# Deferring the norm of the first six tiles to the copies out of PSUM, and spreading the FFN weights' write-backs, in a hybrid decoder layer

## The chip, the cores and the metric

The kernel runs on all 8 cores of one Trainium2 chip. The time is device microseconds (us) of the slowest core. Four cores share a die. A run is called slow when one die is over 1% longer than the other at a lower granted clock, or when the run is over 1.5% above the fastest of the same kernel; such runs occur with many of the kernels here and are left out of all comparisons. Every experiment was timed in rounds with the kernel before on the same chip.

## The reference, cut to what matters

```python
h = rmsnorm(x, g_mix)                 # x * rsqrt(mean(x*x) + eps) * g
proj = h @ w_in                       # q, k, v (512 each), u and qm (256 each)
# three groups of heads read proj: dilated window attention (q, k, v),
# a pooling mixer (u), cross-attention into 256 memory tokens (qm)
x = x + concat(y_attn, y_pool, y_mem) @ w_out
x = x + relu(rmsnorm(x, g_ffn) @ w_ff1) ** 2 @ w_ff2
return rmsnorm(x, g_final)
# x (4, 8192, 1024) float32, D_FF = 4096
```

Each core computes 8 own tiles of 512 tokens. For the window attention it first needs K and V of the 4 tiles that come before them (halo tiles 0 to 3). Tiles 4 to 11 are the core's own.

## The kernel before

The matmuls (PE) take bf16. Weights lie in DRAM as float32 and come in pieces: on first use a piece is loaded with a cast by a DMA of POOL's queue (`ring<-wall`, 2 MB read, 1 MB written), then written back as bf16 by SP's queue (`wscratch<-ring`); later uses load the bf16 copy, again from SP's queue (`ring<-wscratch`, 1 MB). Three slots (the ring) hold the piece in use and two ahead. PE (matmuls; PEld are its weight loads), ACT, DVE and POOL (element by element work) and SP (issues DMAs) each work off one queue in program order; `T.op` and `T.dma` add the waits for semaphores. PE writes to PSUM, from which ACT or DVE copies the result out.

```python
class LN:                                       # cut
    def square(self, k):                        # ACT squares chunk k, DVE adds it to acc
        ...
    def stat(self):                             # PE: mean over features by a float32 matmul with ones
        m_, bm_ = next_mm()
        mm_ops(m_, bm_, [(ones, self.acc, ...)])
        # ACT: acc = exp(-0.5 * ln(m + eps))
    def norm(self, k):                          # DVE: h[k] = x[k] * g[k] * acc
        ...

# ... cut: projections of tile j read h; a copy out of PSUM follows each group of 8 matmuls
for j in range(NHALO):                          # halo tiles
    nxt = stage_A(j + 1)
    side = ln_side(nxt, 0, 0.5, 4, 4.5, 0.5)    # squares, stat, norm of the next tile, between the groups
    groups = stage_B(j)
    if j == 3:                                  # keys and values of the memory tokens
        mln, mg = mem_groups()
        side += ln_side(mln, 2.2, 0.5, 6.2, 6.7, 0.4)
        groups += mg
    run(groups, side)

# V's rows take a turn through DRAM to be permuted; POOL waits for all four and reads them back
def read_v():
    for t_ in toks:
        T.wait("pool", t_)
    T.dma("pool", vsr_sem[j % 2], Vd4[...], vs[...])

# plan of the weights: 18 pieces are cast in the first own tile, 8 of them again in the second
deferred = {P_FF1 + i for i in range(1, 8, 2)} | {P_FF2 + i for i in range(1, 8, 2)}
def ring_issue():
    # ... cut
    if idx in done:
        T.dma("sp", ring_sem[s], ring[s][:], sc[idx], ...)
    else:
        T.dma("pool", cast_sem[s], ring[s][:], wall[idx], ...)
        if idx in deferred:
            deferred.discard(idx)
            return                              # no write-back this time
        done.add(idx)
        T.dma("sp", wb_sem[s], sc[idx], ring[s][:], ...)   # SP waits here until the cast has landed
```

The softmax here doesn't subtract the row's maximum and nothing guards it: scores larger than these inputs give would overflow.

## Time and profile before

Before: median 1656.29 us (3 runs, 1654.83 to 1660.23). The profiled run is core 1, the slowest. The page's head, busy times, chain and DMA issues ("us to landing" is the median from issue to landing):

```profile
span 1660.2 us, 27812 instructions; the slowest of 8 cores (1640.5 to 1660.2 us)
PE 1548.5 (93%) x9722; PEld 748.0 (45%) x9722; DVE 930.2 (56%) x1383; ACT 715.5 (43%) x1069; POOL 137.2 (8%) x189
...
PE 80%; DMA 7%; DVE 5%; issue 4%; ACT 4%; ACTq 0%; DVEq 0%; POOL 0%; SPq 0%; POOLq 0%
...
ring<-wscratch SPq DMA_DIRECT2D x142, 1024.0 KB, 5.9
ring<-wall POOLq DMA_DIRECT2D x29, 1024.0 KB, 12.0
```

PE is busy 93% of the span and 80% of the chain that ended last. The gain has to come from PE's idle time and from time at a lower clock. The waits of PE show the idle time (total, times, longest):

```profile
PE mm L336 <- DVE acc L362: 38.9, 8, 19.5
PE mm L336 <- DVE X L709: 15.9, 13, 1.5
PE mm L336 <- DMA ring<-wall: 9.9, 3, 4.7
PE mm L336 <- DMA ring<-wscratch: 9.4, 2, 7.3
```

39 us are waits for sums of squares (`acc`), of which 19.5 come before the first tile; 19 us are waits for weights. The timeline of PE shows the start (start, duration, what, in brackets the idle time before and what ended it):

```profile
19.53 2.05 PE L336 MATMUL mm<-acc,ones 128*128 128x512 f32 x2 [19.53 <-DVE acc L362]
24.05 11.38 PE L336 MATMUL mm<-ring,hT 128*128 128x512 bf16 x32 [2.48 <-DVE hT L374]
38.06 2.05 PE L336 MATMUL mm<-acc,ones 128*128 128x512 f32 x2 [2.62 <-DVE acc L362]
...
115.39 7.07 PE L336 MATMUL mm<-hT,ring 128*128 128x512 bf16 x32
...
147.96 0.60 PE L554 MATMUL sc<-QM,kmT 64*128 64x512 bf16 x4
```

The first projection is at 24.05 us, the first own tile's at 115.39, and its attention (`sc<-QM`) starts at 147.96.

### The profile page before, as it was taken

Reading aid. Unit: us, or ns where it says so; the run is one execution under the profiler, and the core shown is the slowest. Engines: PE = TensorE matmul, PEld = TensorE weight load, DVE = VectorE, ACT = ScalarE, POOL = GpSimd, SP = SyncE. Lnnn points to the kernel's source line nnn. Section 1 sums busy time; section 2 is a strip of 40 time slices with the busy share of each in tenths; the row PEclk is TensorE's granted clock in tenths of the full one; section 3 lists DMA queues with packets and bytes.
Section 4 is the critical chain, followed back from the end, with each engine's and each line's share of the span. In section 5 each row is a group of like instructions: output and inputs, shape, how many; then the busy total and the mean of one; then the engine's idle time right before and its main releaser. Section 6 shows DMA issues by size and latency. Waiting matters only on the chain.

```text
span 1660.2 us, 27812 instructions; the slowest of 8 cores (1640.5 to 1660.2 us)
## 1 busy us (share of the span) xinstructions
PE 1548.5 (93%) x9722; PEld 748.0 (45%) x9722; DVE 930.2 (56%) x1383; ACT 715.5 (43%) x1069; POOL 137.2 (8%) x189
## 2 busy tenths in 40 slices
PE   3889899989799999999999999999999999998996
PEld 1434544444355444454454444454445444453442
DVE  5666566546365466656465556656565555546333
ACT  3545654532444336443444436343444335442221
POOL 1102110101000010000100010000100000000000
PEclk9999999999999999999999999999999999998998
DMA  9828578995857675354835375344734373434342
GB/s 227 227 87 263 131 153 165 198 203 174 245 152 201 180 219 200 105 176 138 276 107 178 110 233 178 128 153 166 253 114 167 128 234 122 163 130 152 139 152 90
DMA packets 41081, 282.93 MB, mean 170 GB/s; under 512 B 5248, under 2 KB 5376, under 8 KB 8560
## 3 DMA queue, kind: packets, MB, share of 16 engines
q1 hardware_dynamic: 24048, 172.01, 30.6%
q0 software_dynamic: 16896, 109.13, 25.6%
q8 instruction: 81, 1.33, 0.3%
q14 instruction: 56, 0.46, 0.1%
HBM read 266.77 MB, written 46.92 MB: 189 GB/s over the span
## 4 chain that ended last, share of the span: by engine, by line
PE 80%; DMA 7%; DVE 5%; issue 4%; ACT 4%; ACTq 0%; DVEq 0%; POOL 0%; SPq 0%; POOLq 0%
PE mm L336 70%; PE ob L577 6%; PE sc L554 4%; DMA ring<-wall 3%; DMA ring<-wscratch 2%; ACT P L556 2%; DVE acc L362 1%; ACT sq L360 1%; DMA wscratch<-ring 1%; DVE val L588 1%; DMA out<-X 1%; DVE X L709 1%; DVE X L374 0%; DMA cpc_t<-cpc 0%; ACT rt L686 0%
## 5 line engine op out<-in xcount | busy, mean ns | idle before, releaser
L336 PE MATMUL mm<-h2T,ring 128*128 128x512 bf16 x2192 | 511.0, 383 | 13.9 <-DMA ring<-wscratch 7.3
L336 PE MATMUL mm<-aT,ring 128*128 128x512 bf16 x2048 | 474.2, 382 | 24.5 <-DVE X L709 15.9
L689 DVE TENSOR_TENSOR aT<-rt 128x512 bf16<-128x512 f32 x256 | 199.9, 783 | 242.6 <-ACT rt L686 241.1
L556 ACT ACTIVATE P<-sc 128x1024 bf16<-128x1024 f32 x256 | 247.7, 1023 | 184.4 <-PE sc L554 178.7
L336 PEld LDWEIGHTS mm<-h2T,ring 128*128 128x128 bf16 x2192 | 206.7, 98 | 256.3 <-issue 32.7
L336 PEld LDWEIGHTS mm<-aT,ring 128*128 128x128 bf16 x2048 | 192.6, 98 | 249.5 <-issue 42.8
L686 ACT ACTIVATE rt<-mm 128x512 f32<-128x512 f32 x256 | 153.0, 598 | 272.2 <-PE mm L336 250.7
L561 DVE TENSOR_TENSOR P<-P,E 128x1024 bf16<-128x1024 bf16 x224 | 154.0, 694 | 127.6 <-ACT P L556 126.5
L360 ACT ACTIVATE sq<-X 128x512 f32<-128x512 f32 x196 | 122.4, 630 | 161.3 <-DVE X L709 102.5
L362 DVE TENSOR_TENSOR acc<-acc,sq 128x512 f32<-128x512 f32 (+1 forms) x203 | 142.9, 705 | 73.6 <-ACT sq L360 71.1
L336 PE MATMUL mm<-hT,ring 128*128 128x512 bf16 x704 | 156.3, 383 | 0.5 <-DVE KT L343 0.5
L709 DVE TENSOR_TENSOR X<-X,mm 128x512 f32<-128x512 f32 x128 | 87.6, 685 | 119.2 <-PE mm L336 118.6
L577 PE MATMUL ob<-P,Vd 128*128 128x128 bf16 x1792 | 136.7, 219 | 9.6 <-DVE val L588 7.8
L577 PEld LDWEIGHTS ob<-P,Vd 128*128 128x128 bf16 x1792 | 116.1, 98 | 64.9 <-issue 20.9
L592 POOL TENSOR_TENSOR yT<-val,den 128x512 bf16<-128x512 f32 x48 | 62.4, 1300 | 772.6 <-DVE val L588 240.0
L336 PE MATMUL mm<-yT,ring 128*128 128x512 bf16 x512 | 114.8, 383 | 2.7 <-POOL yT L592 2.1
L336 PEld LDWEIGHTS mm<-hT,ring 128*128 128x128 bf16 x704 | 69.2, 99 | 87.2 <-issue 8.2
L336 PEld LDWEIGHTS mm<-yT,ring 128*128 128x128 bf16 x512 | 49.8, 98 | 68.4 <-issue 12.3
L374 DVE SCALAR_TENSOR_TENSOR h2T<-X,gc,acc 128x512 bf16<-128x512 f32 x88 | 61.7, 745 | 27.8 <-ACT acc L370 23.5
L554 PE MATMUL sc<-Q,KT 64*128 64x128 bf16 x1792 | 71.8, 219 | 2.0 <-ACT P L556 1.3
L588 DVE COPY val<-ob 64x512 f32<-64x512 f32 x96 | 65.9, 687 | 13.1 <-PE ob L577 11.1
L336 PE MATMUL mm<-ring,hT 128*128 128x512 bf16 x288 | 68.6, 389 | 3.1 <-DVE hT L374 2.5
(70 smaller groups left out, 785.1 us busy)
## 6 DMA issues: line engine op xcount, KB each, us to landing
ring<-wscratch SPq DMA_DIRECT2D x142, 1024.0 KB, 5.9
ring<-wall POOLq DMA_DIRECT2D x29, 1024.0 KB, 12.0
X<-xh POOLq DMA_DIRECT2D x24, 1024.0 KB, 10.5
wscratch<-ring SPq DMA_DIRECT2D x21, 1024.0 KB, 7.3
X<-xr POOLq DMA_DIRECT2D x16, 1024.0 KB, 7.1
out<-X POOLq DMA_DIRECT2D x16, 1024.0 KB, 9.9
Vd<-vscratch POOLq DMA_DIRECT2D x10, 768.0 KB, 7.8
vscratch<-Vd POOLq DMA_DIRECT2D x32, 192.0 KB, 7.1
```

Of the source, the lines that this page charges most:

```text
L336: T.op("pe", lambda: nc.tensor.matmul(out_ap, lhsT=l, rhs=r, start=(i == 0), stop=(i == n - 1)), reads=rd, writes=[b_out], mark=(i == n - 1))
L360: T.op("act", lambda: nc.scalar.activation(out=s_, in_=self.x3[:, k, :], func=AF.Square), reads=[self.b_x[k]], writes=[bs_])
L362: T.op("dve", lambda: nc.vector.tensor_tensor(out=self.acc, in0=self.acc, in1=s_, op=ALU.add), reads=[bs_], writes=[self.b_acc])
L554: T.op("pe", lambda: nc.tensor.matmul(o2, lhsT=l[lo:lo + 64], rhs=rr, start=True, stop=True), reads=bt["qk_reads"], writes=[bs_], mark=(i ...
L556: T.op("act", lambda: nc.scalar.activation(out=P_[:], in_=s_[:], func=AF.Exp, scale=0.125), reads=[bs_], writes=[bP_])
L561: T.op("dve", lambda: nc.vector.tensor_tensor(out=Pv, in0=Pv, in1=m, op=ALU.mult), reads=[bP_, b_E, b_E16], writes=[bP_])
L577: T.op("pe", lambda: nc.tensor.matmul(o_, lhsT=l[:, v0:v0 + 128], rhs=r_, start=(bt["first"] and i == 0), stop=(bt["last"] and i == n - 1) ...
L588: T.op("dve", lambda: nc.vector.tensor_copy(out=val[lo:lo + 64, :], in_=ob[hh][lo:lo + 64, :]), reads=[b_ob[hh]], writes=[b_val[hh]])
L592: T.op("pool", lambda: nc.gpsimd.tensor_tensor(out=yT[:, ch, :], in0=val[:], in1=den[:], op=ALU.mult), reads=b_den + b_val, writes=[b_yT[ch]])
L686: T.op("act", lambda: nc.scalar.activation(out=rt[i][:, 0:TOK], in_=m_[:], func=AF.Relu), reads=[bm_], writes=[b_rt[i]])
L689: T.op("dve", lambda: nc.vector.tensor_tensor(out=aT[:, a_, :], in0=rt[i][:, 0:TOK], in1=rt[i][:, 0:TOK], op=ALU.mult), reads=[b_rt[i]], w ...
L709: T.op("dve", lambda: nc.vector.tensor_tensor(out=xi[:, d, :], in0=xi[:, d, :], in1=m_[:], op=ALU.add), reads=[bm_], writes=[bxi[d]])
```

## The change

It has two halves.

1. The start. The projections of tiles 0 to 5 take x times the gain, with no norm, so that PE need not wait for the sum of squares. The reciprocal norm is multiplied in at the copies out of PSUM: along the free axis for K, Q and U (DVE, `tensor_tensor` with acc), per partition for V (ACT's scale), for which four one-column float32 matmuls per tile (the column statistics) make a column form of the norm. V of a halo tile runs chunk by chunk, a third input buffer lies in `aT`, V's weights load first, the memory tokens' work moves into the first own tile, and there the pooling mixer's additions go from DVE to POOL.
2. The plan of weights. Instead of 10 write-backs in the first own tile and 8 in the second there are 4, 5, 5 and 4 in the first four, at the price of 19 more cast loads. The load of the next x moves from step 11.7 to 17.

The diff, cut to its core:

```diff
-        deferred = {P_FF1 + i for i in range(1, 8, 2)} | {P_FF2 + i for i in range(1, 8, 2)}
+        turn = dict(zip([P_FF1 + i for i in range(4)] + [P_FF2 + i for i in range(4)]
+                        + [P_FF1 + 4 + i for i in range(4)] + [P_FF2 + 4 + i for i in range(4)],
+                        [2, 1, 3, 2, 1, 0, 3, 2, 1, 3, 1, 2, 3, 0, 2, 1]))
 ... (ring_issue)
+            T.dma("pool", cast_sem[s], ring[s][:], wall[idx], writes=[b_ring[s]])
+            if turn.get(idx, 0) == j - NHALO:
                 done.add(idx)
                 T.dma("sp", wb_sem[s], sc[idx], ring[s][:], reads=[b_ring[s]], writes=[b_scp[idx]])
 ... (LNEarly, the norm of tiles 0 to 5)
+            def gain(self, k):      # even k: ACT, out3[k] = x[k] * g; odd k: DVE
+            def stat(self):
+                for b in range(4):
+                    mm_ops(ob[0][:, b:b + 1], b_ob[0], [(a4[:, b, :], ones[:, 0:1], ...)])
+                ... (ACT: col = exp(-0.5 * ln(ob + eps)))
+                LN.stat(self)
 ... (copies out of PSUM, tiles 0 to 5)
+                T.op("act", lambda: nc.scalar.activation(out=d4[:, :, 0::2, :], in_=src, func=AF.Copy,
+                                                         scale=rcol[j % 2][:, b:b + 1]), ...)     # V
+                    T.op("dve", lambda: nc.vector.tensor_tensor(out=out, in0=m_, in1=a_, op=ALU.mult), ...)
 ... (pool_steps)
+                e = "pool" if first_own else "dve"
+                ops.append(lambda: T.op(e, lambda: T.eng[e].tensor_tensor(out=out, in0=in0, in1=in1, op=ALU.add), ...
 ... (first own tile)
+        side = [(0.5, lns[j].stat)]
+        side += [(8, ... write_back(p_) for p_ in (P_V, P_K, P_UM, P_Q)])]
+        side += ln_side(mln, 1, 0.4, 5, 5.5, 0.4)
+            side += gains(lns[j + 1], 8, 0.6) + sums(lns[j + 1], 8.3, 0.6) + [(16, lns[j + 1].stat)]
+        side += [(4 + 0.7 * i, f) for i, f in enumerate(pool_steps(j))]
+        run(stage_B(j) + mg, side)
 ... (own tiles)
-                side += [(11.7, lambda j=j: load_x("pool", (j + 1) % 2, xh[j + 2]))]
+                side += [(17, lambda j=j: load_x("pool", (j + 1) % 2, xh[j + 2]))]
```

A number before a step is its place in a list: step 8 is issued ahead of the group of matmuls with index 8.

## The prediction

> **What bounds it now.** PE is busy 93% of the span (page, part 1) and is 80% of the chain of waits. From 560 to 1500 us it is busy 923 of 940 us (windows): nothing to win there. The loss is in two places.
>
> (a) The start. The PE timeline of core 1 has the first projection at 24.05 us; halo tiles and memory keys end at 115.4; attention of the first own tile starts at 147.96. At 1.73 us per group of eight matmuls the projections are about 91 us of PE. PE waits for the sum of squares 32 us: 19.5 before the first tile, 2.4 to 4.1 in each later one, because squares, sums, statistic and normalisation stand in line. DMA isn't the limit after the first tile: four 2 MB inputs landed by 31.8 us, about 6.3 us each, then input loads waited for buffers (POOL behind hT, 39 us).
>
> (b) The first two own tiles. Waits for weights on core 1: 1.9, 4.7, 3.3, 7.3, 2.1 us between 341 and 548; other cores 7 to 18 us in all. Cast loads take 12 us in the median, up to 20, with write-backs beside them. After such gaps the granted clock was 0.5 for 3.4 to 10 us. "TensorE: Matmul & The Clock Gate", Part 1, of the Trainium skill says that the gate halves the clock after an idle window of 3.4 us; the trace agrees. Such stretches cost core 1 some 8 us more.
>
> **What changes.** Projections start from x times gain (one short op per chunk); the norm is applied when PSUM is copied out; V runs chunk by chunk. V's weights load first. At 6.3 us each I expect them at about 12.5 us, x's halves at 15.7 and 19, K at 25, the second x at 32, the third at 38. The first projection starts near 16.5 instead of 24. Then PE should run nearly gapless: 13.9 us per halo tile plus about 1.7 for statistics (four one-column fp32 matmuls are added to the 1.1 us one). Memory keys (4 us) move into the first own tile. Halo ends near 89, attention starts at 125 to 130 instead of 148. I take off some, because in the first own tile nearly all PSUM copies go to DVE (about 0.7 us each, beside sums, gains and memory norms), and pool sums to POOL (1.3 us each). Gain: 19 us (14 to 25).
>
> Write-backs: 10 in the first own tile become 4; in exchange 19 more cast loads (2 MB read, not 1) in own tiles two to four. DMA share is 0.5 to 0.7 there, so most hide; some may land late beside input loads. Moving the x load from step 11.7 to 17 takes it away from the store. I expect weight waits and slow clock to fall by half to two thirds on the slow cores: 15 us (3 to 22).
>
> Attention, FFN and the end keep their work.
>
> **Time.** 1656 - 19 - 15 = 1622 us, range 1606 to 1640. Faster by over 2% (below 1623.2): 0.54; within 2%: 0.44; slower: 0.02.
>
> **What would show it.** First projection near 16.5 us; PE waits for sums below 5 us after it; attention of the first own tile at 125 to 130; waits for weights below 8 us on the slowest core, none over 4; at most two steps of clock 0.5 between 100 and 500; 48 casts instead of 29, and no new waits for weights after 560; the end's length unchanged.
>
> **What would make it wrong.** PE waits for DVE in the first own tile (K and Q copies late); slow one-column fp32 matmuls; POOL's small copies at the start delaying the third halo input; cast loads of tiles two and three landing late, which turns (b) into new waits.

## More of the kernel before

In each own tile the pieces come in this order: W_out 0 and 1, the projections V, K, Q, U of the next tile, then FF1 pieces 0 to 3, FF2 0 to 3, FF1 4 to 7, FF2 4 to 7. When a piece has been used up, the piece three places on is issued into its slot.

The weight waits stand in the first two own tiles. This part of the chain is at the border between projections and FFN in the second (start, duration, what):

```profile
412.95 9.27 DMA out<-X
...
423.33 12.24 DMA ring<-wall
...
435.64 0.32 SPq L100
...
436.12 15.29 DMA ring<-wscratch
...
451.65 4.51 PE mm L336 x14
```

It reads: a store of the last tile lands; then POOL issues a cast load (FF1 piece 1), which lands 12.24 us later; only then does SP issue that piece's write-back, and behind it the load of piece 2; PE gets piece 2 at 451.65.

## The result, and the profile after

The changed kernel took 1681.71 us (median of 4 runs; three fast ones at 1679.03 to 1684.28 and a slow one at 1830.0) against 1658.26 for the kernel before (4 runs). The ratio is 1.0137, 95% interval 1.0102 to 1.0173. Ratios here and below are the mean time of one kernel's fast runs over that of the other's of the same rounds, so they are not quite the ratios of the medians. The prediction of 1622 (1606 to 1640) was wrong in sign.

The same views of the slowest core, again core 1, first the page:

```profile
span 1678.1 us, 27902 instructions; the slowest of 8 cores (1659.5 to 1678.1 us)
PE 1556.4 (93%) x9770; PEld 757.5 (45%) x9770; DVE 924.1 (55%) x1363; ACT 718.0 (43%) x1079; POOL 160.2 (10%) x230
...
PE 78%; DMA 8%; DVE 5%; ACT 4%; issue 4%; POOL 0%; ACTq 0%; DVEq 0%; POOLq 0%; SPq 0%
...
ring<-wscratch SPq DMA_DIRECT2D x123, 1024.0 KB, 5.6
ring<-wall POOLq DMA_DIRECT2D x48, 1024.0 KB, 10.8
```

48 cast loads instead of 29, as foreseen. Each takes a little less in the median, 10.8 us. The waits of PE:

```profile
PE mm L353 <- DMA ring<-wall: 19.8, 5, 6.7
PE sc L353 <- ACT hT L411: 17.9, 1, 17.9
PE mm L353 <- DVE X L816: 15.9, 13, 1.5
PE mm L353 <- DVE KT L582: 13.8, 6, 7.9
PE mm L353 <- DMA ring<-wscratch: 9.5, 1, 9.5
PE mm L353 <- DVE acc L384: 6.6, 2, 4.0
```

The waits for sums at the start are gone but for 5.3 us under other names (2.8 for the column statistics, 2.5 for the memory tokens); the 6.6 us shown stand at the end of the kernel, and stood there before. New are 13.8 us for copies of K out of PSUM, one of 7.9 us, and the waits for weights grew from 19 to 29 us. The timeline of PE at the start:

```profile
17.86 9.25 PE L353 MATMUL sc<-ring,hT 128*128 128x512 bf16 x32 [17.86 <-ACT hT L411]
26.99 2.00 PE L353 MATMUL ob<-ones,acc 128*128 128x1 f32 x8
28.85 1.11 PE L353 MATMUL mm<-acc,ones 128*128 128x512 f32 x2
...
44.44 2.00 PE L353 MATMUL ob<-ones,acc 128*128 128x1 f32 x8 [0.67 <-DVE acc L384]
...
81.24 0.95 PE L353 MATMUL ob<-ones,acc 128*128 128x1 f32 x8
...
100.58 1.89 PE L353 MATMUL sc<-hT,ring 128*128 128x512 bf16 x8
...
139.38 6.46 PE L353 MATMUL mm<-hT,aT 128*128 128x512 bf16 x16 [7.89 <-DVE KT L582]
...
155.09 0.61 PE L660 MATMUL sc<-QM,kmT 64*128 64x512 bf16 x4
```

The first own tile's projections begin at 100.58 instead of 115.39, but its attention only at 155.09 instead of 147.96: 54.5 us for a stretch that took 32.6 before (there without the memory tokens, whose matmuls are about 5 us). Now split the span by stage. The first projection of own tile j's output (`yT,ring`) marks the beginning of a tile's stage I; the table has the mean over the 8 cores of the profiled run, in us, worked out from the trace.

| | before | after |
|---|---|---|
| attention of first own tile starts | 147.5 | 153.4 |
| its output projection starts | 201.1 | 206.7 |
| from there to the second tile's | 171.9 | 169.1 |
| second to third | 198.1 | 198.3 |
| third to fourth | 185.1 | 202.4 |
| each later tile but the last | 185.1 to 185.4 | 185.1 to 185.2 |
| mean span of the cores | 1649.1 | 1669.3 |

So of 20.2 us, 5.9 come from the start, 17.3 from the third own tile, and the first own tile gave 2.8 back. The rows from the second tile on run to the output projection of the next tile, so "third" covers output projection and FFN of own tile 3, with the projections of tile 4 between them.

Where the start loses can be added up. From the first projection to the attention of the first own tile, mean of the 8 cores, before took 123.0 us and after 135.1:

| | before | after | cost |
|---|---|---|---|
| PE idle | 16.8 | 20.0 | +3.2 |
| PE busy at granted clock 0.5, after the first clock record | 7.5 | 12.2 | +2.4 (half of it) |
| PE busy before the first clock record, taken as half speed too | 7.3 | 4.5 | -1.4 (half) |
| the six tiles' column statistics, at full clock | 0 | 7.9 | +7.9 |
| the ordinary statistics, at full clock (before, tile 0's lies ahead of this stretch) | 4.7 | 5.6 | +1.0 |
| all other matmuls, at full clock | 94.1 | 93.3 | -0.9 |
| sum | | | +12.2 |

The head start was 6.2 us (first projection at 24.5 before and 18.3 after, mean of the cores), and 6.2 less 12.2 is the loss of about 6. The largest entry is the column statistics. In tiles 3 to 5 they took 0.95 to 0.97 us, in tiles 0 to 2 2.00 us (1.81 once), on every core, and the granted clock was 1.0 when they began. What differs in the program is the operand: in tiles 0 to 2 the matmul takes every fourth column of `acc` as its weights, later a contiguous block, and a weight load took 327 ns there against 192 later. No run tested another layout, or left the column statistics out.

The Trainium skill, "TensorE: Matmul & The Clock Gate", Part 1, says that the array runs at half clock after at least one idle window of about 3.4 us. This trace agrees in the sizes (records of 0.5 for 3.4, 6.8 and 10.2 us), but such records also came after much less idle time. On core 1 the clock was 0.5 from 46.2 us on, and in the 3.4 us before PE had been idle for 0.67 us only, while column statistics took 1.76. Of the 15 records of 0.5 before 75 us on the eight cores, 8 came like this: under 1 us idle, and 1.6 to 2.0 us of column statistics. So these may cost clock as well as time; that is seen side by side in the trace and not tested.

The chain through the longest wait at the start:

```profile
123.51 8.76 DMA vscratch<-Vd
...
132.81 0.54 POOL Vd L100
...
133.41 1.07 POOL rt L711
...
137.08 1.27 POOL rt L711
...
138.44 0.06 DVE rt L727
...
138.54 0.70 DVE KT L582
...
139.38 6.48 PE mm L353 x16
```

V's last rows take 8.76 us to land in DRAM. POOL waits for them (`read_v`), and only then reaches the pooling additions (`rt`), the last of which ends at 138.35. DVE's next instruction needs their result. Behind it in DVE's queue stands K's copy, which has nothing to do with pooling, and PE waits for that copy's PSUM buffer.

And the chain at the border in the third tile:

```profile
614.43 15.78 DMA ring<-wall
...
630.29 0.32 SPq L100
...
630.76 18.72 DMA ring<-wscratch
...
649.73 5.59 PE mm L353 x16
```

It is the pattern of before, one piece earlier. FF1 piece 0 (turn 2) is now a cast load from POOL's queue. Its slot was free when K's last group ended, near 611.1 us (worked out: the 96 matmuls of K, Q and U took 20.88 us from 604.14 on, K's are the first third), but POOL issued the load at 614.43, behind its wait for V's rows (landed at 612.27), their read-back and a store; the load then ran beside that store and the x load, and landed after 15.78 us, 4.8 us late for PE. Its write-back waited for it in SP's queue, and behind the write-back stood the load of piece 1, which was issued at 630.76 and landed 18.72 us later: another 9.5 us. In the kernel before, piece 0 at the same place in the second tile came as bf16 from SP's queue: by the trace it was issued at 409.80 and landed at 415.59. So the cast load is late by its issue (3.3 us) and by its own length (15.78 us, 10.8 in the median); no run separates the two.

### The profile page after: what moved, and what is told of

The parts are those of the page before. It is cut to its first block, busy times and chain, and to the rows that moved or that the text cites. A ratio compares the mean times of both kernels' runs of the same rounds, so it can differ in the third digit from the quotient of the medians.

```text
span 1678.1 us, 27902 instructions; the slowest of 8 cores (1659.5 to 1678.1 us)
## 1 busy us (share of the span) xinstructions
PE 1556.4 (93%) x9770; PEld 757.5 (45%) x9770; DVE 924.1 (55%) x1363; ACT 718.0 (43%) x1079; POOL 160.2 (10%) x230
## 3 DMA queue, kind: packets, MB, share of 16 engines
q0 software_dynamic: 19632, 129.05, 32.6%
## 4 chain that ended last, share of the span: by engine, by line
PE 78%; DMA 8%; DVE 5%; ACT 4%; issue 4%; POOL 0%; ACTq 0%; DVEq 0%; POOLq 0%; SPq 0%
PE mm L353 66%; PE ob L683 6%; DMA ring<-wall 5%; PE sc L660 4%; PE sc L353 2%; ACT P L662 2%; DMA ring<-wscratch 1%; DMA vscratch<-Vd 1%; DVE val L694 1%; DMA X<-xh 1%; DVE acc L384 1%; DMA out<-X 1%; DVE X L396 1%; DVE X L816 1%; DVE h2T L396 1%
## 5 line engine op out<-in xcount | busy, mean ns | idle before, releaser
L353 PE MATMUL mm<-h2T,ring 128*128 128x512 bf16 x2192 | 516.5, 385 | 31.5 <-DMA ring<-wall 14.7
L796 DVE TENSOR_TENSOR aT<-rt 128x512 bf16<-128x512 f32 x256 | 202.4, 792 | 261.4 <-ACT rt L793 260.1
L353 PE MATMUL mm<-hT,ring 128*128 128x512 bf16 x672 | 147.0, 379 | 2.6 <-DVE KT L582 2.5
L384 DVE TENSOR_TENSOR acc<-acc,sq 128x512 f32<-128x512 f32 x144 | 104.4, 725 | 41.2 <-ACT sq L374 40.5
L353 PEld LDWEIGHTS mm<-hT,ring 128*128 128x128 bf16 x672 | 65.4, 98 | 83.0 <-issue 6.2
L694 DVE COPY val<-ob 64x512 f32<-64x512 f32 x96 | 65.9, 687 | 12.7 <-PE ob L683 10.7
L660 PEld LDWEIGHTS sc<-Q,KT 64*128 64x128 bf16 x1792 | 53.6, 107 | 40.0 <-issue 36.7
L692 ACT ACTIVATE den<-ob 64x512 f32<-64x512 f32 x96 | 56.8, 592 | 29.4 <-PE ob L683 27.4
## 6 DMA issues: line engine op xcount, KB each, us to landing
ring<-wall POOLq DMA_DIRECT2D x48, 1024.0 KB, 10.8
```

The lines of the kernel that those rows point to most:

```text
L353: T.op("pe", lambda: nc.tensor.matmul(out_ap, lhsT=l, rhs=r, start=(i == 0), stop=(i == n - 1)), reads=rd, writes=[b_out], mark=(i == n - 1))
L384: T.op("dve", lambda: nc.vector.tensor_tensor(out=self.acc, in0=self.acc, in1=s_, op=ALU.add), reads=[bs_], writes=self.b_acc)
L660: T.op("pe", lambda: nc.tensor.matmul(o2, lhsT=l[lo:lo + 64], rhs=rr, start=True, stop=True), reads=bt["qk_reads"], writes=[bs_], mark=(i ...
L694: T.op("dve", lambda: nc.vector.tensor_copy(out=val[lo:lo + 64, :], in_=ob[hh][lo:lo + 64, :]), reads=[b_ob[hh]], writes=[b_val[hh]])
L796: T.op("dve", lambda: nc.vector.tensor_tensor(out=aT[:, a_, :], in0=rt[i][:, 0:TOK], in1=rt[i][:, 0:TOK], op=ALU.mult), reads=[b_rt[i]], w ...
```

## The experiments

The theories. For the start, R1: the order in POOL's queue, as just read, blocks DVE and through it PE. R2: DVE itself is too full in the first own tile, since nearly all copies out of PSUM are now DVE's. R3: POOL and DVE hinder each other. For the third tile, T1: the wrong pieces are cast at the border, where POOL's and SP's queues are blocked. T2: 19 more cast loads simply overload DMA.

Results, with the mean over the cores of the attention's start and of own tiles 1 to 3 from the profiled run. The first two lines are the first measurement. The kernel before, in the rounds of b1 to b4, has one run of 1678.31 among others of 1656.53 to 1658.35; it counts as fast, widens these four intervals and lowers their ratios by about 0.2%.

| run | mean of fast runs | ratio to before (95%) | attention | tiles 1, 2, 3 |
|---|---|---|---|---|
| before | 1658.0 | 1 | 147.5 | 171.9, 198.1, 185.1 |
| changed | 1680.8 | 1.0137 (1.0102 to 1.0173) | 153.4 | 169.1, 198.3, 202.4 |
| e1_sums_dve | 1672.1 | 1.0079 (1.0059 to 1.0098) | 150.4 | 168.5, 197.1, 202.9 |
| e2_sums_pool_early (wrong) | 1676.7 | 1.0106 (1.0082 to 1.0129) | 153.7 | 169.1, 197.6, 203.1 |
| e3_old_turns | 1664.9 | 1.0035 (1.0013 to 1.0057) | 153.2 | 172.2, 198.2, 185.4 |
| e4_turns_permuted | 1649.3 | 0.9950 (0.9918 to 0.9981) | 153.5 | 169.1, 185.3, 187.6 |
| b1_before_ring | 1668.9 | 1.0052 (0.9979 to 1.0124) | 147.7 | 167.1, 196.3, 203.1 |
| b2_before_ring_permuted | 1640.9 | 0.9878 (0.9819 to 0.9937) | 147.5 | 167.1, 185.8, 189.0 |
| b3_permuted_sums_dve | 1646.2 | 0.9910 (0.9849 to 0.9971) | 151.3 | 168.3, 186.5, 189.9 |
| b4_permuted_pool_early | 1647.4 | 0.9917 (0.9846 to 0.9988) | 152.3 | 168.1, 185.2, 188.5 |
| e6_writeback_late | 1677.5 | 1.0100 (1.0080 to 1.0120) | 151.1 | 168.1, 199.9, 204.4 |
| v1_balanced | 1643.1 | 0.9896 (0.9872 to 0.9920) | 146.2 | 168.7, 185.6, 189.4 |
| v2_balanced_plain5 | 1646.7 | 0.9914 (0.9889 to 0.9940) | 150.1 | 166.8, 186.2, 189.7 |
| b5_before_ring_spread | 1638.6 | 0.9866 (0.9847 to 0.9885) | 148.4 | 167.5, 185.3, 185.2 |
| h1_after_late | 1673.1 | 1.0080 (1.0058 to 1.0103) | 154.9 | 169.8, 199.6, 196.5 |
| h4_one_swap | 1658.9 | 1.0001 (0.9981 to 1.0021) | 154.8 | 169.4, 193.5, 186.7 |
| h3_b5_late | 1637.7 | 0.9867 (0.9851 to 0.9883) | 147.9 | 167.3, 185.7, 185.2 |
| h2_v1_spread_late | 1639.4 | 0.9878 (0.9858 to 0.9898) | 146.8 | 169.0, 185.8, 185.2 |

### e1_sums_dve: the pooling additions back on DVE

```diff
-                e = "pool" if first_own else "dve"
+                e = "dve"
```

> The changed kernel with one edit: the additions of the pooling mixer for the first own tile go back from POOL to DVE. Theory R1 (order in POOL's queue): in the changed kernel four additions stand in POOL's queue behind a wait for the landing of V's rows in DRAM (132.8 us), DVE's in-order queue waits for them (7.3 us idle), and with it K's copy out of PSUM, so PE stands 7.9 us and then runs at half clock for 10 us. Without it that wait is gone, attention of the first own tile starts at 140 to 146 us instead of 149 to 157, and the kernel is 8 to 12 us faster than the changed one (about 1671). Rival R2 (DVE is overloaded in this tile, since it now makes nearly all copies out of PSUM): DVE gets 4 us more work, attention starts at 155 or later, total the same or some us longer.

The total fell by 9 us and, by ratio, by 0.6%; the mean over the cores fell by only 4.1 (1669.3 to 1665.2), of which the attention's start gives 3.0. The 7.9 us wait for K is gone; its slowest core waits like this between 95 and 160 us:

```profile
PE mm L353 <- DVE KT L582: 5.3, 5, 1.3
PE mm L353 <- DVE val L384: 2.6, 1, 2.6
PE mm L353 <- DVE dT L733: 1.5, 1, 1.5
PE mm L353 <- DVE Q L582: 1.2, 2, 0.6
```

Five waits for K now make 5.3 us, none over 1.3. So R1 holds for the one long wait, but the attention started at 148 to 154 us, not at 140 to 146: more than half of R1's expected gain came back as short waits for a DVE with more to do, as R2 has it.

### e2_sums_pool_early: the additions on POOL, but earlier in its queue

```diff
-        side += [(4 + 0.7 * i, f) for i, f in enumerate(pool_steps(j))]
+        side += [(4 + 0.2 * i, f) for i, f in enumerate(pool_steps(j))]
```

> The changed kernel with one edit: the pooling steps of the first own tile are emitted closer together (0.2 instead of 0.7 of a group apart), so that POOL's additions stand in its queue before the wait for V's rows, and stay on POOL. R1 (queue order): the same gain as with the additions on DVE, attention starts at 140 to 146 us, total 8 to 12 us less than the changed kernel. R2 (DVE overload): attention start unchanged within 2 us, 149 to 157. Rival R3 (POOL and DVE slow each other when both read SBUF): the variant with DVE gains, this one doesn't.

The result was wrong (relative error 0.042), by a mistake of mine: the two map matmuls among the steps write into the tile that still holds the memory tokens, and at the closer spacing they came before those had been read. Nor did it gain at the start: the attention began at 152 to 156 us, because the maps now stood early in PE's queue, where PE waited 9.6 us for their operand. The wait had only moved. It decides nothing between R1 and R2; b4 mends it.

### e3_old_turns: the write-backs as before, the rest as changed

```diff
-                        [2, 1, 3, 2, 1, 0, 3, 2, 1, 3, 1, 2, 3, 0, 2, 1]))
+                        [0, 1, 0, 1, 0, 1, 0, 1, 0, 1, 0, 1, 0, 1, 0, 1]))
```

> The changed kernel with the old plan of write-backs (even FFN pieces in the first own tile, odd ones in the second; no cast loads later); everything else stays. T1 (head of line: a write-back waits in SP's queue for a late cast load and holds up the next weight load) and T2 (plain DMA overload by 19 more cast loads) both expect the third own tile back at 185 us from 199 to 205, the first own tile up by 0 to 8 us on some cores, the second within 5 us. Total 8 to 14 us less than the changed kernel, about 1670.

As expected: the third tile is back at 185.4, the first rises by 3.1, the second stays. The total fell by some 16 us, 2 more than expected. What is left over before (ratio 1.0035) is the start. This run keeps the x load at step 17, so with the old plan of weights that move by itself costs nothing.

### e4_turns_permuted: the same counts, other pieces

```diff
-                        [2, 1, 3, 2, 1, 0, 3, 2, 1, 3, 1, 2, 3, 0, 2, 1]))
+                        [0, 0, 1, 1, 1, 1, 1, 2, 3, 3, 2, 2, 3, 3, 2, 2]))
```

> The changed kernel with the same number of cast loads and write-backs in each own tile (2, 5, 5, 4 written back), but other pieces: FF1 pieces 0 and 1, the first after the border between projections and FFN, are written back in the first own tile, pieces 2 and 3 in the second, so that in the third tile the first pieces come from the bf16 copy. T1 (head of line at that border): third own tile 185 to 190 us instead of 199 to 205, total 10 to 15 us less than the changed kernel. T2 (overload by bytes): the waits appear beside the later cast loads, third tile 197 to 205, total within 4 us of the changed kernel.

Just as many cast loads and write-backs in each tile, and 31 us less than the changed kernel: twice what T1 expected, because the second tile lost its waits too (198.3 to 185.3), which the kernel before has as well. T2 falls: with the same bytes per tile, what matters is which piece has to come through POOL's queue at the border. That DMA is crowded just there is not excluded.

### b1_before_ring and b2_before_ring_permuted: the plan alone

Edit: the kernel before with the code of `turn` from the diff above and the x load at step 17; b1 has the turns of the change, b2 those of e4.

> The kernel before with only the changed plan of write-backs (the turns of the change) and the x load at step 17: the second half of the change alone. If the plan itself is at fault, the third own tile takes 199 to 205 us instead of 185, as in the changed kernel, the first own tile 168 to 171 instead of 167 to 181, and the total is 4 to 16 us over the kernel before. If the plan hurts only together with the earlier start, the total is below the kernel before.

> The kernel before with the permuted plan (2, 5, 5, 4 write-backs, but the FFN's first pieces early) and the x load at step 17. Head-of-line theory: first own tile 168 to 171 us, second 185 (from 196 to 201), third 185 to 190; total 18 to 25 us under the kernel before, 1633 to 1640, and some 10 us under the changed kernel with the same plan, as the changed start reaches the first own tile's output projection 5 us later. If the plan's gain belongs to the changed start, total within 10 us of the kernel before.

b1 has the third tile at 203.1 us: the plan is at fault by itself. Its total has a wide interval (1.0052, 0.9979 to 1.0124), so I go by the cores' mean spans: e3 (the start alone) is 5.3 us over before, b1 (the plan alone) 12.7, and both together, the changed kernel, 20.2; the two halves roughly add up. b2 came out at 1640.9, 17 us under before's median (1658.15), and 8 us under the changed kernel with the same plan (e4), some 10 being expected: the changed start is a loss with a good plan as well.

### b3_permuted_sums_dve and b4_permuted_pool_early

Edits: e4 with e1's; and e4 with this, so that the additions come before `read_v` and the maps late:

```diff
-        side += [(4 + 0.7 * i, f) for i, f in enumerate(pool_steps(j))]
+        side += [(4 + 0.2 * i if i < 15 else i + 0.0, f) for i, f in enumerate(pool_steps(j))]
```

> The changed kernel with the permuted plan and the pooling sums on DVE, two edits that gained 31 and 9 us alone. If they are independent, 1640 to 1644; attention of the first own tile starts at 148 to 154 us, third own tile 185 to 190.

> The changed kernel with the permuted plan; the pooling sums stay on POOL but are emitted before the wait for V's rows, and, other than in the wrong run, the two map matmuls and the margin copy come late (steps 15 to 16), after the memory norms have been read from the tile that they overwrite. Queue-order theory: no wait of PE over 3 us for DVE in the first own tile, attention starts at 141 to 147 us, total 1636 to 1642; the result is correct. If POOL and DVE hinder each other, or DVE is simply full, attention starts at 149 or later and the total is 1646 or more.

b3 gained 3.1 us over e4 instead of 9, and b4 1.9, with a correct result; the cores' mean spans differ by +1.0 and -1.2 us, so neither gain is shown. The attention began at 152.3 in b4 and the total is over 1646, which was expected for the rivals and not for R1 alone. In b4's slowest core PE still waited 7.3 us for K. DVE stood idle for 5.0 us before that, waiting for an addition of POOL: the additions, though now ahead of `read_v` in POOL's queue, still had two writes of V's rows between them, which wait for DVE's instructions (POOL stood idle for 3.0 us before the one at 121.79). So my queue-order theory was too narrow. It isn't one wait in POOL's queue, but a chain that alternates between two in-order queues. R3 was not isolated by any run; the additions took 1.06 to 1.27 us each in the changed kernel's chain above.

### e6_writeback_late: the 4 MB of projection weights written later

```diff
-        side += [(8, lambda: [T.wait("sp", ...)] + [write_back(p_) for p_ in (P_V, P_K, P_UM, P_Q)])]
+        side += [(20, lambda: [T.wait("sp", ...)] + [write_back(p_) for p_ in (P_V, P_K, P_UM, P_Q)])]
```

> The changed kernel with one edit: the write-backs of the four projection weights (4 MB) are put at the end of the first own tile's projections instead of step 8. POOL's queue order stays. If the long landing of V's last rows (123.5 to 132.3 us) comes from those writes, it falls to 2 to 4 us as for the first rows, POOL's sums start near 127 instead of 133, PE's longest wait for a copy of K falls from 7.9 to under 3 us, and the total is 5 to 9 us under the changed kernel (1673 to 1677), nearly what putting the sums on DVE gave. If POOL's own order alone is at fault, attention start and total stay within 3 us.

The link is confirmed: V's last rows now landed after 2.1 us (120.91 to 123.04), and the longest wait for K in this tile was 1.7 us. The attention's start fell by 2.3 us in the mean. By ratio the total fell by 0.4% (1.0137 to 1.0100), about 6 us and as expected, by the means of fast runs by 3; but the cores' mean span stayed (1669.3 and 1670.0), because the second and third tiles were 1.6 and 2.0 us longer in this run's profile. The gain at the start is shown, that of the total isn't. The expectation allowed less than 3 us for both if POOL's own order alone was at fault, so the slow landing is a link in the long wait and not the whole loss.

### v1_balanced and v2_balanced_plain5: less for DVE at once

Edit of v1, on b3: the memory tokens' squares, norm and matmuls back in halo tile 3, and

```diff
-            side += gains(lns[j + 1], 8, 0.6) + sums(lns[j + 1], 8.3, 0.6) + [(16, lns[j + 1].stat)]
+            side += gains(lns[j + 1], 1, 0.6) + sums(lns[j + 1], 1.3, 0.6) + [(9, lns[j + 1].stat)]
```

v2 normalises the second own tile before its projections, as before, with squares, statistic and norm in steps 1 to 13.5.

> The changed kernel with the permuted plan, sums on DVE, the memory tokens' work moved back to the last halo tile, and the gains and squares of the second own tile started 7 groups earlier: it tests whether DVE's crowding in the second half of the first own tile is what remains of the loss at the start. If so, PE's waits for K, Q and dT in that tile (about 8 us with the sums on DVE) fall below 3 us, attention of the first own tile starts at 139 to 144 us, total 1630 to 1636, faster than every kernel so far. If the remaining loss is elsewhere (halo tiles, statistics), attention starts at 148 or later and the total is 1641 or more.

> The same, but the second own tile is normalised before its projections, as in the kernel before; so its Q copies go back to ACT and 2.7 us of DVE work go. Within 3 us of the balanced one if DVE is no longer full there; 3 to 6 us faster if it still is.

v1 brought the attention to 146.2 us, 5.1 better than b3, so DVE's crowding was a part (R2). From first projection to attention it took 127.7 us: PE idle 12.9 (20.0 in the changed kernel), clock 0.5 for 11.5 (17.1). The attention's start is only 1.3 us ahead of the kernel before; 139 to 144 us were expected, and a total of 1630 to 1636 where 1643.1 was measured. PE idle and clock 0.5 together now cost no more than in the kernel before (16.8 and 7.7); what stays is the column statistics, 8.1 us in this run, and short waits for copies. v2 was worse by 3.9 us at that point; on its slowest core PE waited 4.3 us for the sum of squares, which I had placed too early in PE's queue.

### b5_before_ring_spread, h3_b5_late

b5 is b2 with turns `[0, 0, 1, 1, 1, 1, 2, 3, 0, 1, 2, 3, 0, 2, 3, 2]`. h3 is b5 with the late write-backs described next.

> The kernel before with another plan: the same first pieces as in the permuted plan, and of the pieces that load beside the residual input (FF1 pieces 4 to 7, FF2 piece 4) one or two written back per tile instead of two or three in the third and fourth. If write-backs and casts beside that input cause the 2 to 7 us left in the third tile, it falls to 185 to 187 and the total is 1634 to 1638; else 1641.

> The kernel before with the spread plan (1639 us) and the late write-backs. Tiles are already at 167 to 169, 185 and 185; within 3 us of 1639, since no weight wait is left for it to take away.

The tiles came as expected, b5's total (1638.6) just above the 1634 to 1638 hoped for. b5 does not only choose other pieces: it writes back 6, 5, 4 and 3, which makes 43 cast loads instead of 48. The second and third own tiles are now within 0.7 us of the later ones' 185.1. b5 (0.9866) and h3 (0.9867) are the fastest versions found: the start of the kernel before with a better plan.

### h1_after_late and h4_one_swap: which link at the border?

h1 puts each write-back into SP's queue one weight issue later:

```diff
             if idx in done:
                 T.dma("sp", ring_sem[s], ring[s][:], sc[idx], ...)
+                flush()                      # emits the write-backs in `late`
                 return
+            flush()
             T.dma("pool", cast_sem[s], ring[s][:], wall[idx], writes=[b_ring[s]])
             if turn.get(idx, 0) == j - NHALO:
                 done.add(idx)
-                T.dma("sp", wb_sem[s], sc[idx], ring[s][:], ...)
+                late.append((s, idx))
```

h4 exchanges two turns and nothing else:

```diff
-                        [2, 1, 3, 2, 1, 0, 3, 2, 1, 3, 1, 2, 3, 0, 2, 1]))
+                        [0, 1, 3, 2, 1, 2, 3, 2, 1, 3, 1, 2, 3, 0, 2, 1]))
```

> The changed kernel, its turns kept, with each FFN write-back put into SP's queue one weight issue later, after the next load. If SP's queue order is the main link, the 9.5 us wait for piece 1 in the third own tile goes, and what stays is the wait for piece 0 (about 5 us and some half clock): third tile 188 to 194 us instead of 199 to 205, total 8 to 14 us under the changed kernel. If the late cast of piece 0 and crowded DMA are the main link, third tile 198 or more, total within 4 us.

> The changed kernel with two turns exchanged: FF1 piece 0 is written back in the first own tile and FF2 piece 1 in the third. Same counts of casts and writes in each tile. Both links at the border go for the third tile: 185 to 189 us instead of 199 to 205; second tile 190 to 198 (its piece 1 is still a cast with a write-back). Total 14 to 20 us under the changed kernel. If crowding by bytes were the cause, nothing changes.

h1: third tile 196.5 (188 to 194 expected, 198 or more for the rival), 5.9 us of 17.3; the wait for the bf16 copy (`wscratch`) is gone, but on its slowest core piece 0 now lands 19.27 us after its issue. h4: third tile 186.7, second 193.5, and the total 22 us below the changed kernel, level with before (1.0001). The waits of PE from 560 to 700 us, in the changed kernel, h1 and h4, each on its slowest core:

```profile
PE mm L353 <- DMA ring<-wscratch: 9.5, 1, 9.5
PE mm L353 <- DMA ring<-wall: 4.8, 1, 4.8
```

```profile
PE mm L361 <- DMA ring<-wall: 9.8, 1, 9.8
```

```profile
PE mm L353 <- DMA ring<-wscratch: 1.2, 1, 1.2
```

So the root is the late cast load of one piece, taken away with its write-back by h4. SP's queue order makes it worse, by about a third of the loss.

### h2_v1_spread_late: everything repaired

Edit: v1 with b5's turns and the late write-backs.

> The balanced start (attention of the first own tile at 144 to 150 us) with the spread plan and late write-backs. Each tile 168 to 170, 185, 185; then the total differs from the run with the start of before by the start alone: 0 to 3 us faster, 1634 to 1639. If it is 1641 or more, the changed start costs something later that is not seen yet.

The runs were 1637.90, 1640.98 and two slow ones of 1661.39 and 1912.75; ratio 0.9878 (0.9858 to 0.9898), from two fast runs. Beside h3 on the same chip (0.9867) there is no gain: the attention starts 1.1 us earlier, the first own tile takes 1.7 us longer. The early start is worth nothing that these runs can show, even when repaired.

## Why the prediction was wrong

- Right: where PE lost time before; the 48 cast loads; the landing times at the start. V's weights, x's halves, K and the third x were expected at 12.5, 15.7 and 19, 25 and 38 us; the trace of core 1 has 12.02, 15.57 and 18.81, 25.34 and 37.87. The first projection came at 17.9 instead of 16.5, waits for sums nearly vanished, and the length of all tiles after the third did not change.
- Wrong: "Then PE should run nearly gapless: 13.9 us per halo tile plus about 1.7 for statistics", and with it "attention starts at 125 to 130". It started at 155.1 on core 1. The halo tiles ended at 100.6 instead of 89, and the first own tile took 54.5 us instead of the 36 to 41 implied. I had named DVE's load there and taken "some" off. The sum that was left out is the one in the table: 7.9 us of column statistics, and idle time and half clock that did not fall but rose by 4.2 us together. The 1.7 us held in tiles 3 and 4 (1.75 for both statistics, start to start) but not in tiles 0 to 2 (2.6 to 3.7), which "slow one-column fp32 matmuls" in the prediction's list of dangers had named. And a dependence on the sum of squares was replaced by a dependence on DVE's and POOL's queues: e1, e6 and v1 each moved the attention forward, by 2.3 to 5.1 us, by loosening it.
- Wrong: "DMA share is 0.5 to 0.7 there, so most hide". Bytes had room, as e4 shows with the same counts; but the share is an average over a tile and says nothing about a piece that is due 14 us after its slot came free (611.1 to 625.6), at a place where the issuing queue is blocked and a store and an x load run beside. The expected 15 us of gain became 2.8 in the first tile, nothing in the second, and a loss of 17.3 in the third.
- Wrong by omission: I read the 7.3 us wait at 451 us as crowded DMA ("with write-backs beside them"). The chain of before showed already that the write-back in SP's queue waited for a late cast. Had I followed which piece each turn puts at that border, I would have seen turn 2 on the first FFN piece.

Still open: how much of the half clock at the start follows from the waits and how much from the column statistics, what the start is worth without these, how much of the late cast load is late issue and how much crowded DMA, and whether POOL's and DVE's accesses hinder each other. No run separated these.

## What to carry to other kernels

In this kernel, a load that goes into an in-order queue behind other waits was as late as the slowest of them, and everything behind it in the next queue inherited the delay; so choose by due time which transfers may take the slow path, and put them where queues are quiet, rather than counting bytes per stage. A change that removes one dependence of PE must be costed with the queues on which PE will then depend, engine by engine, over the stretch where they bunch. Look also at how a small added operation reads its operand: here the same column statistics took 0.95 or 2.00 us. Before moving work to an idle engine, look at what stands in front of it in that engine's queue.

## What the Trainium skill lacked or had wrong

- "DMA: Bandwidth & Descriptors", section "SWDGE vs HWDGE vs iDMA", states that a DMA that casts can only be issued by GpSimd; all 48 cast loads stand in POOL's queue. It doesn't say what that costs when POOL also waits for other data: here a cast load was issued at 614.43 us for a slot free near 611.1, and keeping piece 0 out of that queue, in exchange for one piece that is due elsewhere, gave 15.7 us in the third tile (202.4 to 186.7).
- The same page, "Issuing engines are not separate DMA queues", counts only the sequencer's time to initiate a DMA as the use of several issuing engines. What this passage lacks is that an issuing engine in order also holds back later DMAs while it waits: one write-back that waited for a cast load held the next weight load until 630.76 us, and moving it back by one place in SP's queue gave 5.9 us.
- "TensorE: Matmul & The Clock Gate", "Back-to-back issue gap", gives about 131 ns per matmul as the sustained spacing at N=512 with weight loads in the stream. 32 matmuls of 128x512 with their weight loads took 7.07 us at full clock, about 220 ns each, near its figure for the isolated gap (216 ns); from start to start (29.79 to 36.70) it is 216 ns.
- The same page, Part 1, has half clock after an idle window of 3.4 us; here half clock was also recorded from 46.2 us on core 1, after 3.4 us with only 0.67 us idle and 1.76 us of one-column statistics. The table there names idle windows, not how busy a window has to be.
